# Gate and up projections of a feed-forward as seven products of half blocks, with the down projection moved behind them

## The chip, the cores and the metric

The kernel runs on one core of a Trainium2 chip. The metric is the device time of one execution in microseconds; the median of three runs is compared. All matrix products run on TensorE (PE in the profile), which takes a stationary operand of 128 x 128 and a moving one of up to 512 columns and adds into banks of PSUM. VectorE (DVE), ScalarE (ACT) and GpSimd (POOL) do the elementwise work, and the queue of SyncE (SP) issues the transfers between DRAM and SBUF.

## The reference

One layer of a streaming encoder over 1024 tokens of width 1024: two kinds of attention, a gated merge and an output projection, and then the feed-forward that this change is about:

```python
        merged = jax.nn.sigmoid(g_a) * y_a + jax.nn.sigmoid(g_b) * y_b
        x = x + rms_norm(merged @ w_o[l], ln_mix_post[l])

        h = rms_norm(x, ln_ffn_pre[l])
        f = (jax.nn.silu(h @ w_ffn_gate[l]) * (h @ w_ffn_up[l])) @ w_ffn_down[l]
        x = x + rms_norm(f, ln_ffn_post[l])
```

All of it is float32. The inner width of the feed-forward is 2816, 22 tiles of 128 (f tiles), and the model width is 8 tiles of 128 (k tiles).

## The kernel before

Every float32 matrix that is multiplied is held as two parts in a format that TensorE reads faster, a high and a low one. The high part is a cast on ACT (L252), the low part is what the cast left out, a subtract on POOL or DVE (L254); from PSUM it is L258 and L259. A product of two such matrices is three matmuls: high by high (L265), high by low (L266), low by high (L267). `load_hl` (L279) loads a matrix from DRAM (L283) and splits it.

The program runs in stages: norm and input projection, both attentions, `branch` a and b (projection of each attention, times its gate), `mix_out` (output projection and the two norms around it), then `ffn_gate_up` and `ffn_down`, and `finish` for each token tile. SBUF is one tensor AR for split parts and one tensor AFm for raw data; a `Zone` hands out places in them, of the free room the longest unused first. A scheduler orders each engine's queue; an instruction waits in its queue for what it reads and for the place that it writes.

`mix_out` goes over eight token tiles. One is 8 k tiles x 2 halves x 3 matmuls of 512 columns, and then a chain: sum of squares on ACT (L1062), reciprocal root (`rstd`: DVE L243, POOL L245), DVE L1064 and L1066, ACT L1069, `rstd` again, DVE L1071. The result is transposed on PE (L1085) and split into `h2`, the moving operand of the feed-forward. The transposes of a tile (the function `late`) are issued behind the matmuls of the next tile, and those of the last tile are handed to the feed-forward as `hook`, behind its first 48 matmuls.

`ffn_gate_up` works on a pair of f tiles (11 pairs). For each half of the tokens and each f tile it runs gate and up, 8 k tiles x 3 matmuls each, then Silu on ACT (L1116), the multiply on DVE (L1118) and a split into `aa`, which stays in SBUF. `ffn_down` multiplies `aa` of one or two such pairs with their rows of the down weights, 8 token tiles x 2 halves, and adds into a sum in SBUF (L1143, L1145). Gate and up of the next pair and down of the ones before alternate; the last group has four f tiles.

Of the kernel before, what the change touches and what calls it, by code (L numbers as in the profile page):

```python
# [65 lines left out]
MLA_DEPTH = 2  # L66

# [7 lines left out]
class Mem:  # L75
    """Columns of one SBUF tensor, handed out in program order."""
# [15 lines left out]
class Zone:  # L92
    """Windows of a Mem; of the room that is free there, the longest unused goes first."""
# [46 lines left out]
class Banks:  # L140
    """A window of PSUM banks; one bank, or an even and the next one, the longest unused first."""
# [27 lines left out]
def kernel(  # L169
# [46 lines left out]
    s_x1 = scratch("s_x1", (S, D))  # L216

# [19 lines left out]
    # ---------------------------------------------------------------- helpers  # L237
# [31 lines left out]
    class HL:  # L269
        """A matrix tile held as high and low parts: .h and .l of the given free shape."""  # L270
# [19 lines left out]
    # ------------------------------------------------------------ zones of phase one  # L290
# [18 lines left out]
    # ------------------------------------------------------------ phase 0: rotary tables  # L309
# [55 lines left out]
    def rope(src, t, nb, mid, dst):  # L365
        """dst = rope(src) for nb blocks of 64 columns; the tables of `mid` (q scaled, k plain, or both)."""
# [912 lines left out]
```

## Time and profile before

| | us |
|---|---|
| median of 3 runs | 2069.7 |
| lowest and highest | 2068.66, 2070.66 |
| span of the profiled execution, first to last instruction | 2069.1 |
| PE busy | 2027.3 |
| DVE, ACT, POOL busy | 1009.0, 784.5, 443.4 |
| wait of PE at the start of `mix_out` | 2.9 |
| waits of PE around the start of the feed-forward | 5.5 |

Of the profiled execution the span is what is given; it lies 0.6 us below the median of the runs. Busy times are sums over stages of different kinds: attention ends at about 1080 us, `branch` at about 1240, `mix_out` at about 1332, and the rest is the feed-forward. A matmul's printed duration (0.39 us for 512 columns) is longer than the distance between two starts, because consecutive matmuls overlap.

### The profile page before, as it was taken

How to read it: one execution, taken by the hardware profiler on the slowest of the kernel's cores; microseconds unless marked ns; L12 is line 12 of the kernel's file. 1: busy time of each engine (PE TensorE's matmuls, PEld its weight loads, DVE VectorE, ACT ScalarE, POOL GpSimd, SP SyncE). 2: the span in 40 equal slices, each digit the busy share in tenths (PEclk: the TensorE clock that was granted, in tenths of full speed). 3: DMA queues.
4: the chain of work that ended last, by engine and by line, in shares of the span. 5: the costliest groups of instructions: out<-in, count | busy, mean ns of one | idle time of the engine just before them, and what ended most of it. 6: DMA issues, size and time to landing. Idle time of an engine off the chain costs nothing.

```text
span 2069.1 us, 28932 instructions
## 1 busy us (share of the span) xinstructions
PE 2027.3 (98%) x10920; PEld 1762.1 (85%) x10920; DVE 1009.0 (49%) x2283; ACT 784.5 (38%) x1734; POOL 443.4 (21%) x559
## 2 busy tenths in 40 slices
PE   6999999999999999999999999999999999999998
PEld 6898999999898988988888887878888888888886
DVE  7756757766665667877733364412122221222115
ACT  5435445454544446666753332321211112111112
POOL 2000010200000022222121221332323323133225
PEclk9999999999999999999999999999999999999999
DMA  5212121120211131440335434210212112121114
GB/s 166 74 40 82 42 61 44 55 62 28 78 45 59 49 105 46 158 145 19 107 92 158 141 115 141 88 56 31 62 31 61 52 40 60 33 61 42 51 41 142
DMA packets 138987, 153.44 MB, mean 74 GB/s; under 512 B 12480, under 2 KB 116320, under 8 KB 138848
## 3 DMA queue, kind: packets, MB, share of 16 engines
q1 hardware_dynamic: 138848, 151.60, 23.7%
q8 instruction: 85, 1.39, 0.3%
q14 instruction: 54, 0.44, 0.1%
HBM read 119.00 MB, written 32.57 MB: 73 GB/s over the span
## 4 chain that ended last, share of the span: by engine, by line
PE 89%; DVE 3%; ACT 2%; issue 1%; DMA 1%; POOL 1%; POOLq 0%; DVEq 0%; SPq 0%; ACTq 0%
PE PS L265 26%; PE PS L267 26%; PE PS L266 26%; PE PS L702 3%; PE PS L604 3%; PE PS L920 2%; DVE AR L254 1%; POOL AR L254 1%; DVE nm L643 0%; PE PS L684 0%; ACT AFm L644 0%; ACT AR L252 0%; PE PS L685 0%; PE PS L587 0%; PE PS L747 0%
## 5 line engine op out<-in xcount | busy, mean ns | idle before, releaser
L265 PE MATMUL PS<-AR 128*128 128x512 f32 (+3 forms) x2920 | 1070.5, 368 | 2.9 <-ACT AR L252 1.3
L266 PE MATMUL PS<-AR 128*128 128x512 f32 (+3 forms) x2920 | 1058.6, 363 | 3.1 <-DVE AR L254 2.9
L267 PE MATMUL PS<-AR 128*128 128x512 f32 (+3 forms) x2920 | 1059.8, 364 | 1.1 <-POOL AR L254 1.1
L265 PEld LDWEIGHTS PS<-AR 128*128 128x128 f32 x2920 | 550.6, 189 | 82.3 <-ACT AR L258 3.9
L266 PEld LDWEIGHTS PS<-AR 128*128 128x128 f32 x2920 | 551.3, 189 | 74.5 <-DVE AR L254 3.4
L267 PEld LDWEIGHTS PS<-AR 128*128 128x128 f32 x2920 | 550.3, 189 | 71.9 <-POOL AR L254 1.5
L252 ACT CAST AR<-AFm 128x1024 fp32r<-128x1024 f32 (+5 forms) x366 | 236.9, 670 | 567.0 <-PE PS L266 247.3
L254 POOL TENSOR_TENSOR AR<-AFm,AR 128x1024 fp32r<-128x1024 f32 (+4 forms) x169 | 298.3, 1774 | 690.4 <-ACT AR L252 644.7
L1118 DVE TENSOR_TENSOR AFm<-AFm,PS 128x512 f32<-128x512 f32 x44 | 30.3, 688 | 440.4 <-PE PS L267 438.4
L258 ACT CAST AR<-PS 128x512 fp32r<-128x512 f32 (+3 forms) x336 | 143.3, 447 | 149.2 <-DVE AFm L383 75.5
L259 DVE TENSOR_TENSOR AR<-PS,AR 128x512 fp32r<-128x512 f32 (+3 forms) x336 | 164.3, 506 | 39.4 <-ACT AR L258 37.9
L254 DVE TENSOR_TENSOR AR<-AFm,AR 128x384 fp32r<-128x384 f32 (+4 forms) x197 | 131.0, 696 | 78.7 <-ACT AR L252 51.7
L644 ACT ACTIVATE AFm<-PS,nm 128x1024 f32<-128x1024 f32 (+3 forms) x192 | 142.7, 745 | 46.0 <-DVE nm L643 28.8
L643 DVE TENSOR_REDUCE nm<-PS 128x1 f32<-128x1024 f32 (+3 forms) x192 | 143.7, 752 | 3.2
L1145 DVE TENSOR_TENSOR AFm<-AFm,PS 128x512 f32<-128x512 f32 x144 | 99.0, 688 | 94.6 <-PE PS L267 94.6
L614 POOL CAST AR<-AR 128x128 fp32r<-128x128 f32 (+1 forms) x128 | 43.8, 342 | 455.7 <-PE PS L685 262.3
L702 PE MATMUL PS<-AR 128*128 128x256 f32 x640 | 95.0, 290 | 0.1
L604 PE MATMUL PS<-idf,AFm 128*128 128x128 f32 x576 | 88.6, 275 | 2.2 <-ACT AFm L736 1.1
L702 PEld LDWEIGHTS PS<-AR 128*128 128x128 f32 x640 | 82.1, 189 | 5.2 <-ACT AFm L644 2.3
L622 POOL MEMSET AR<- 128x256 f32 x64 | 22.4, 350 | 294.0 <-PE PS L267 198.9
L604 PEld LDWEIGHTS PS<-idf,AFm 128*128 128x128 f32 x576 | 66.9, 140 | 10.8 <-ACT AFm L946 4.3
L1116 ACT ACTIVATE AFm<-PS 128x512 f32<-128x512 f32 x44 | 26.3, 597 | 127.8 <-PE PS L267 127.8
(121 smaller groups left out, 1242.5 us busy)
## 6 DMA issues: line engine op xcount, KB each, us to landing
AFm<-in_w_in_dram SPq DMA_DIRECT2D x72, 192.0 KB
AFm<-in_w_ffn_gate_dram SPq DMA_DIRECT2D x22, 512.0 KB
AFm<-in_w_ffn_up_dram SPq DMA_DIRECT2D x22, 512.0 KB
AFm<-in_w_ffn_down_dram SPq DMA_DIRECT2D x22, 512.0 KB
AFm<-in_x_dram SPq DMA_DIRECT2D x16, 512.0 KB
AFm<-in_w_in_dram SPq DMA_DIRECT2D x32, 256.0 KB
s_gate<-AFm SPq DMA_DIRECT2D x32, 256.0 KB
AFm<-s_gate SPq DMA_DIRECT2D x16, 512.0 KB
```

Source lines behind the costliest of these rows:

```text
L252: nc.scalar.copy(h, src)
L254: e.tensor_tensor(out=l, in0=src, in1=f32v(h), op=ALU.subtract)
L258: nc.scalar.copy(h, src)
L259: nc.vector.tensor_tensor(out=l, in0=src, in1=f32v(h), op=ALU.subtract)
L265: nc.tensor.matmul(o, lhsT=sh, rhs=mh, start=first, stop=False)
L266: nc.tensor.matmul(o, lhsT=sh, rhs=ml, start=False, stop=False)
L267: nc.tensor.matmul(o, lhsT=sl, rhs=mh, start=False, stop=last)
L604: nc.tensor.transpose(tb.ap[:, q * P:(q + 1) * P], C[:, (g + q) * P:(g + q + 1) * P], idf)
L643: nc.vector.tensor_reduce(out=nm[:, m:m + 1], in_=src, axis=ax, op=ALU.max, negate=True)
L644: nc.scalar.activation(out=dst, in_=src, func=ACTF.Exp, bias=nm[:, m:m + 1], scale=1.0, accum_out=ss[:, m:m + 1])
L702: nc.tensor.matmul(sb.ap[:, p * 256:(p + 1) * 256], lhsT=qs.ap[:, m * 256 + v * P:m * 256 + v * P + P], rhs=slots[p]["kT"][:, m, :], start ...
L1145: nc.vector.tensor_tensor(out=acc, in0=acc, in1=pb.ap, op=ALU.add)
```

## The change

For a pair of f tiles of gate (or up), the product of weights and `h2` is seen as a product of 2 x 2 blocks: two f tiles by two halves of k, and two halves of k by two halves of the tokens. By Strassen's method in Winograd's form these blocks are multiplied in seven products of half size in place of eight, each of 4 k tiles x 3 matmuls of 512 columns; sums and differences of blocks are made before and after.

- The weight parts (`stationary_parts`): seven per pair and projection, four sums or differences of raw blocks (three on DVE, one on POOL) and seven splits (five subtracts on POOL, two on DVE). Six parts are made ahead of use.
- The moving parts (`moving_parts`): for each of four pairs of token tiles, four differences (three on DVE, one on POOL) and seven splits (three on POOL, four on DVE), made in `mix_out` once both tiles of a pair are transposed. `mix_out` takes the token tiles in the order 0, 4, 1, 5, 2, 6, 3, 7. A moving operand is now four runs of 128 columns that lie 7168 columns apart, since the parts of the four pairs stand behind one another.
- After the products: a copy from PSUM on ACT and five adds on DVE per block; Silu on ACT for gate, the multiply for up (one on DVE, three on POOL), and the result is stored to DRAM (`s_aa`).
- `ffn_down` runs after all pairs, in groups of 2, 4, 4, 4, 4 and 4 f tiles; it loads `s_aa` and the down weights and splits both.
- The transposes of the last token tile stand behind the first two products (24 matmuls). `branch` b splits its result in four pieces of 128 columns in place of two of 256. The places of several matrices in AR move.

The core of the diff (helpers move two lines down, so L265 to L267 are L267 to L269 after it):

```diff
-    z_oa, z_ob, z_pw, z_mt = slots(mr, (2, 10)), slots(mr, (10, 18)), slots(mr, (0, 2), (18, 19)), [slots(mr, (2 + 2 * q, 4 + 2 * q)) for q in range(4)]
+    z_oa, z_ob, z_pw = slots(mr, (2, 10)), slots(mr, (9, 11), (13, 19)), slots(mr, (0, 3))
+    z_mt = [slots(mr, (q, q + 2)) for q in (3, 5, 7, 11)]
...
-    z_wo, z_h2, z_ff = slots(mr, (10, 18)), slots(mr, (0, 8)), slots(mr, (8, 19))
+    z_wo = [slots(mr, (q, q + 1)) for q in (9, 10, 13, 14, 15, 16, 17, 18)]
+    z_wc, z_dn = Zone(mr, (28672, AR_COLS)), Zone(mr, (0, AR_COLS))
...
+        order = [t for p in range(4) for t in (p, p + 4)]
...
+            def flip():
                 for g in range(2):
                     tb = ps_a.alloc()
                     for i in range(4):
                         k = 4 * g + i
                         nc.tensor.transpose(tb.ap[:, i * P:(i + 1) * P], y.ap[:, k * P:(k + 1) * P], idf)
-                    split_psum(tb.ap.rearrange("p (k s) -> p k s", k=4), h2[:, 4 * g:4 * g + 4, 0, hs], h2[:, 4 * g:4 * g + 4, 1, hs])
+                    b = X.f.alloc(512)
+                    if g:
+                        nc.vector.tensor_copy(b.ap, tb.ap)
+                    else:
+                        nc.scalar.copy(b.ap, tb.ap)
...
+                if t >= 4:
+                    moving_parts(t - 4)
...
+        def moving_parts(p):
+            blk = Zone(mr, (7168 * p, 7168 * (p + 1))).alloc(7168, 7168)
+            v = blk.v("p (i h c) -> p i h c", i=7, h=2)
+            b11, b12, b21, b22 = raw.pop((0, 0)), raw.pop((0, 1)), raw.pop((1, 0)), raw.pop((1, 1))
...
+            put(MB["11"], b11, "pool")
+            put(MB["21"], b21, "dve")
+            t1 = diff(b12, b11, nc.vector)
+            t3 = diff(b22, b12, nc.gpsimd)
+            t2 = diff(b22, t1, nc.vector)
+            put(MB["t1"], t1, "pool")
+            put(MB["t3"], t3, "dve")
+            put(MB["22"], b22, "pool")
+            t4 = diff(b21, t2, nc.vector)
+            put(MB["t2"], t2, "dve")
+            put(MB["t4"], t4, "dve")
...
+    def stationary_parts(wt, g):
+        raw = f_ffn.alloc(2048)
...
+        yield part(A[0, 0], "pool")
+        s1, s1v = both(A[1, 0], A[1, 1], ALU.add, nc.vector)
+        s2, s2v = both(s1v, A[0, 0], ALU.subtract, nc.vector)
+        yield part(s2v, "pool")
+        yield part(s1v, "dve")
+        s3, s3v = both(A[0, 0], A[1, 0], ALU.subtract, nc.gpsimd)
+        yield part(s3v, "pool")
+        yield part(A[0, 1], "pool")
+        yield part(A[1, 1], "pool")
+        s4, s4v = both(A[0, 1], s2v, ALU.subtract, nc.vector)
+        yield part(s4v, "dve")
...
+        def product(bank, i, first):
+            X.fill()
+            w = X.parts.pop(0)
+            v = w.v("p (h k c) -> p h k c", h=2, k=4)
+            for k in range(4):
+                mh, ml = [X.h2v[:, :, i, h, k * P:(k + 1) * P] for h in range(2)]
+                o = bank.ap.rearrange("p (q s) -> p q s", q=4)
+                for x, (ws, m) in enumerate(((0, mh), (0, ml), (1, mh))):
+                    nc.tensor.matmul(o, lhsT=v[:, ws, k], rhs=m, start=first and k == 0 and x == 0,
+                                     stop=k == 3 and x == 2, skip_group_check=True)
...
+                product(a, MB["11"], True)
+                s1 = tmp()
+                nc.scalar.copy(s1.ap, a.ap)
+                product(b, MB["t2"], True)
+                u2 = add(s1, b)
+                product(c, MB["t1"], True)
+                product(b, MB["t3"], False)
+                u3 = add(s1, b)
+                c22 = add(u3, c)
+                done(1, 1, c22)
+                product(a, MB["21"], False)
+                done(0, 0, a)
+                product(b, MB["t4"], False)
+                c21 = add(s1, b)
+                done(1, 0, c21)
+                product(c, MB["22"], False)
+                c12 = add(u2, c)
+                done(0, 1, c12)
+
+    def ffn_down(X, f0, n):
+        aa, ws = [], []
+        for f in range(f0, f0 + n):
+            aa.append(load_hl(s_aa[f * P:(f + 1) * P, :], f_dn, z_dn, S))
+            ws.append(load_hl(w_d[f * P:(f + 1) * P, :], f_dn, z_dn, D, eng="dve"))
...
+    down = [ffn_down(X, 0, 2)] + [ffn_down(X, f0, 4) for f0 in range(2, NFF, 4)]
+    next(down[0])
+    for i, d in enumerate(down):
+        if i + 1 < len(down):
+            next(down[i + 1])
+        next(d, None)
```

How the instructions stand on three engines. First PE before the change, around the transposes of the last token tile (L1085), with feed-forward matmuls (L265 to L267) on both sides:

```order
L266 MATMUL PS<-AR 128x512
L267 MATMUL PS<-AR 128x512
L1085 MATMUL PS<-idf,AFm 128x128 [waits DVE_49]
L1085 MATMUL PS<-idf,AFm 128x128 x7
L265 MATMUL PS<-AR 128x512
L266 MATMUL PS<-AR 128x512
L267 MATMUL PS<-AR 128x512
```

The same place after it: the last matmuls of the output projection (L268, L269), the products (L1216) and the transposes of the last token tile (L1080).

```order
L268 MATMUL PS<-AR 128x512
L269 MATMUL PS<-AR 128x512
L1216 MATMUL PS<-AR 128x512 [waits Activation_49]
L1216 MATMUL PS<-AR 128x512 [waits Pool_49]
L1216 MATMUL PS<-AR 128x512 x10
L1216 MATMUL PS<-AR 128x512 [waits Activation_49]
L1216 MATMUL PS<-AR 128x512 [waits DVE_49]
L1216 MATMUL PS<-AR 128x512 x10
L1080 MATMUL PS<-idf,AFm 128x128 [waits DVE_49]
L1080 MATMUL PS<-idf,AFm 128x128 x7
L1216 MATMUL PS<-AR 128x512 [waits Activation_49]
```

There were 48 matmuls without a wait ahead of these transposes, and there are 24 now, in two products whose first two matmuls wait; the next product behind the transposes waits too.

On DVE the chain of the last token tile before the change, from L1064 to the first multiply of the feed-forward (L1118):

```order
L1064 SCALAR_TENSOR_TENSOR AFm<-PS,rs_r,AFm 128x1024 [waits Pool_49]
L259 TENSOR_TENSOR AR<-PS,AR 128x4x128 [waits Activation_49]
L1066 TENSOR_TENSOR AFm<-AFm 128x1024 [waits DMAHW5_49,DVE_49]
L243 TENSOR_SCALAR rs_v<-ss 128x1 [waits Activation_49]
L1071 SCALAR_TENSOR_TENSOR AFm<-AFm,rs_r 128x1024 [waits Pool_49]
L1118 TENSOR_TENSOR AFm<-AFm,PS 128x512 [waits PE_49,Activation_49]
```

And after it (L1065, L1067 and L1072 are the same three operations; L1180 are sums of raw weights, L1103 and L256 differences and subtracts of the moving parts, L1083 the copy of the transposed tile):

```order
L1065 SCALAR_TENSOR_TENSOR AFm<-PS,rs_r,AFm 128x1024 [waits PE_49,Pool_49]
L1067 TENSOR_TENSOR AFm<-AFm 128x1024 [waits DMAHW5_49,DVE_49]
L1180 TENSOR_TENSOR AFm<-AFm 128x512 [waits DMAHW1_49,DMAHW0_49]
L1180 TENSOR_TENSOR AFm<-AFm 128x512 [waits DVE_49]
L245 TENSOR_SCALAR rs_v<-ss 128x1 [waits Activation_49]
L1072 SCALAR_TENSOR_TENSOR AFm<-AFm,rs_r 128x1024 [waits Pool_49]
L1083 COPY AFm<-PS 128x512 [waits PE_49]
L1103 TENSOR_TENSOR AFm<-AFm 128x512 [waits Activation_49]
L1103 TENSOR_TENSOR AFm<-AFm 128x512 [waits DVE_49]
L256 TENSOR_TENSOR AR<-AFm,AR 128x512 [waits Activation_49]
```

Two sums, of which the first waits for transfers, stand in the chain of the last tile, and behind it the copy and the differences come before the first subtract.

On SP, in the middle of the feed-forward, one pair of f tiles after the change (before it, there were the same weight loads and in place of the stores two loads of down weights):

```order
L1242 DMA s_aa<-AFm 128x512 [waits DMAHW1_49,Pool_49]
L1168 DMA AFm<-in_w_ffn_up_dram 128x4x256 [waits DMAHW2_49,Pool_49]
L1242 DMA s_aa<-AFm 128x512 [waits DMAHW3_49,DVE_49]
L1242 DMA s_aa<-AFm 128x512 [waits DMAHW4_49,Pool_49]
L1242 DMA s_aa<-AFm 128x512 [waits DMAHW5_49,Pool_49]
L1168 DMA AFm<-in_w_ffn_up_dram 128x4x256 [waits DMAHW6_49,DVE_49,Pool_49]
L1168 DMA AFm<-in_w_ffn_gate_dram 128x4x256 [waits DMAHW7_49,Pool_49]
L1168 DMA AFm<-in_w_ffn_gate_dram 128x4x256 [waits DMAHW0_49,DVE_49,Pool_49]
```

Four stores stand among the four weight loads of a pair, and each load waits for POOL, which reads the raw weights that lie in its place.

## Rows read from the trace of the kernel before

**Rows 1.** The page: span, and busy time of each engine

```profile
span 2069.1 us, 28932 instructions
...
PE 2027.3 (98%) x10920; PEld 1762.1 (85%) x10920; DVE 1009.0 (49%) x2283; ACT 784.5 (38%) x1734; POOL 443.4 (21%) x559
```

**Rows 2.** The page: the chain that ended last, by engine

```profile
PE 89%; DVE 3%; ACT 2%; issue 1%; DMA 1%; POOL 1%; POOLq 0%; DVEq 0%; SPq 0%; ACTq 0%
```

**Rows 3.** Waits of PE: 1080 to 1330 us, then 1325 us to the end

```profile
PE PS L266 <- DVE AR L254: 2.9, 1, 2.9
...
PE PS L1085 <- DVE AFm L1071: 5.5, 2, 4.7
```

**Rows 4.** Windows of the feed-forward (columns in the first row)

```profile
core 0: us, PE busy (x) PEld busy (x) DVE busy (x) ACT busy (x) POOL busy (x), PEclk, DMA share, GB/s
1500.00:1600.00 100.00, 100.00 (x443) 82.84 (x442) 23.03 (x34) 15.65 (x20) 27.83 (x14) 1.00 0.16 48
...
1340.00:1380.00 40.00, 35.35 (x152) 29.10 (x151) 9.88 (x10) 9.31 (x14) 10.10 (x7) 0.91 0.19 59
```

**Rows 5.** Timeline of DVE: start us, us, engine, line, operation, idle before

```profile
1363.70 0.69 DVE L1118 TENSOR_TENSOR AFm<-AFm,PS 128x512 f32<-128x512 f32 x1 [9.67 <-PE PS L267]
1374.58 0.69 DVE L1118 TENSOR_TENSOR AFm<-AFm,PS 128x512 f32<-128x512 f32 x1 [10.19 <-PE PS L267]
```

**Rows 6.** Groups by shape, 1080 us to the end

```profile
L254 POOL TENSOR_TENSOR AR<-AFm,AR 128x512 fp32r<-128x512 f32 x44 | 56.7, 1288 | 283.8 <-ACT AR L252 282.1 <-DMA AFm<-in_w_ffn_down_dram 1.7
L1118 DVE TENSOR_TENSOR AFm<-AFm,PS 128x512 f32<-128x512 f32 x44 | 30.3, 688 | 440.4 <-PE PS L267 438.4 <-ACT AFm L1116 2.0
L252 ACT CAST AR<-AFm 128x512 fp32r<-128x512 f32 x44 | 27.3, 620 | 208.5 <-DVE AFm L1118 208.5
...
L1177 POOL TENSOR_TENSOR AFm<-AFm 128x512 f32<-128x512 f32 x14 | 20.9, 1515 | 6.1 <-DVE AFm L1176 6.1
...
L245 POOL TENSOR_TENSOR rs_r<-rs_v,mhalf 128x1 f32<-128x1 f32 x24 | 13.2, 550 | 78.3 <-DVE rs_v L243 78.3
...
L259 DVE TENSOR_TENSOR AR<-PS,AR 128x512 fp32r<-128x512 f32 x16 | 10.9, 684 | 0.9 <-ACT AR L258 0.9
...
L1064 DVE SCALAR_TENSOR_TENSOR AFm<-PS,rs_r,AFm 128x1024 f32<-128x1024 f32 x8 | 10.3, 1284 | 7.6 <-POOL rs_r L245 7.6
...
L1062 ACT ACTIVATE AFm<-PS 128x1024 f32<-128x1024 f32 x8 | 8.2, 1024 | 31.2 <-issue 16.5 <-PE PS L267 14.7
```

**Rows 7.** Timeline of DVE, token tiles of the output projection

```profile
1312.40 1.22 DVE L1066 TENSOR_TENSOR AFm<-AFm 128x1024 f32<-128x1024 f32 x1
...
1315.77 1.28 DVE L1071 SCALAR_TENSOR_TENSOR AFm<-AFm,rs_r 128x1024 f32<-128x1024 f32 x1 [0.73 <-POOL rs_r L245]
...
1346.12 3.35 DVE L1071 SCALAR_TENSOR_TENSOR AFm<-AFm,rs_r 128x1024 f32<-128x1024 f32 x1 [1.36 <-POOL rs_r L245]
```

**Rows 8.** Chain, 1325 to 1360 us: start us, us, what

```profile
1337.46 3.78 DMA AFm<-in_w_ffn_gate_dram
1341.31 1.06 ACT AR L252
...
1342.44 2.38 POOL AR L254
...
1346.12 3.37 DVE AFm L1071
...
1351.50 0.43 PE PS L265
```

**Rows 9.** Timeline of PE, last token tiles of the output projection

```profile
1308.32 1.04 PE L1085 MATMUL PS<-idf,AFm 128*128 128x128 f32 x8
...
1320.12 1.03 PE L1085 MATMUL PS<-idf,AFm 128*128 128x128 f32 x8
...
1331.66 0.39 PE L267 MATMUL PS<-AR 128*128 128x512 f32 x1
...
1349.53 1.97 PE L1085 MATMUL PS<-idf,AFm 128*128 128x128 f32 x8 [4.65 <-DVE AFm L1071]
```

More of the change, by code (lines that the diff above doesn't have):

```diff
@@ L66 @@
 MLA_DEPTH = 2
+AHEAD = 6
 AR_COLS = 38912
@@ L1038, in branch, with mix_out @@
             b.free()
-    def mix_out(X):
-        X.h2 = [None, None]
-        late = None
-        wo = [load_hl(w_o[k * P:(k + 1) * P, :], f_raw, z_wo, D, eng="dve" if k % 2 else "pool") for k in range(NK)]
+    def mix_out(X, prefetch):
+        X.h2 = []
+        wo = [load_hl(w_o[k * P:(k + 1) * P, :], f_raw, z_wo[k], D, eng="dve" if k % 2 else "pool") for k in range(NK)]
         mt = [b.v("p (d h s) -> p d h s", d=NK, h=2) for b in X.mt]
@@ L1047, in mix_out, with post @@
         nc.sync.dma_start(wf.ap, ln_ffn_pre[0].partition_broadcast(P))
[L1048 to L1049 removed]
+        banks = Banks(mp, 0, 6)
+        order = [t for p in range(4) for t in (p, p + 4)]
+        late, raw = [], {}
+        def post(t, pb, xt):
             rows = slice(t * P, (t + 1) * P)
[L1051 to L1059 removed]
             y = X.f.alloc(D, 1024)
@@ new lines, in mix_out @@
+        for n, t in enumerate(order):
+            p, hs = t % 4, slice((t // 4) * P, (t // 4) * P + P)
+            last = n == NT - 1
+            xt = X.f.alloc(D, 1024)
+            nc.sync.dma_start(xt.ap, x2d[t * P:(t + 1) * P, :])
+            pb = banks.alloc(2)
+            ks = (0, 1, 3, 4, 5, 6, 7, 2) if last else range(NK)
+            for x, k in enumerate(ks):
+                for c in range(2):
+                    sl = slice(c * 512, (c + 1) * 512)
+                    mm3(pb.ap[:, sl], mt[p][:, k, 0, hs], mt[p][:, k, 1, hs], wo[k].h[:, sl], wo[k].l[:, sl], x == 0, x == NK - 1)
+                if last:
+                    wo[k].free()
+                    if x == 1:
+                        late.pop(0)()
+                        late.pop(0)()
+                    if x in (3, 5, 6):
+                        prefetch()
+            if n % 2:
+                X.mt[p].free()
+            post(t, pb, xt)
+            if late and n < NT - 2 and len(late) > 1:
+                late.pop(0)()
@@ L1090, in mix_out @@
+        for f in late:
+            f()
         wp.free()
         wf.free()
[L1092 to L1128 removed]
@@ L1241, with prefetch, fill @@
     drain(branch(X, "b"))
-    last_h2 = mix_out(X)
-    X.gu, X.dn = Banks(mp, 0, 4), Banks(mp, 4, 8)
-    X.acc = [X.f.alloc(D, 1024) for _ in range(NT)]
-    prev = []
-    for g in range(NFF // 2):
-        cur = ffn_gate_up(X, g, last_h2 if g == 0 else None)
-        if prev and g < NFF // 2 - 1:
-            ffn_down(X, 2 * g - len(prev), prev)
-            prev = []
-        prev = prev + cur
-    ffn_down(X, NFF - len(prev), prev)
+    X.parts, stream = [], ffn_parts()
+    def prefetch():
+        X.parts.append(next(stream))
+    def fill():
+        while len(X.parts) < AHEAD:
+            b = next(stream, None)
+            if b is None:
+                return
+            X.parts.append(b)
+    X.fill = fill
+    mix_out(X, prefetch)
+    h2 = mr.ap[:, 0:28672]
+    X.h2v = h2.rearrange("p (q i h c) -> p q i h c", q=4, i=7, h=2)
+    ffn_gate_up(X)
+    for b in X.h2:
+        b.free()
+    X.dn = Banks(mp, 0, 8)
+    X.acc = [f_acc.alloc(D, 1024) for _ in range(NT)]
+    down = [ffn_down(X, 0, 2)] + [ffn_down(X, f0, 4) for f0 in range(2, NFF, 4)]
[4 more added lines that the diff above has]
+        next(d, None)
 _INS = ['x', 'positions', 'ln_mix_pre', 'w_in', 'lambda_q1', 'lambda_k1', 'lambda_q2', 'lambda_k2', 'da_subln',
```

144 lines of the change are left out of this document (82 added, 62 removed).

## The prediction

> **What bounds the kernel now.** I read the page first: TensorE is busy in 2027.3 of 2069.1 us [rows 1], and it is 89% of the chain that ended last [rows 2]. A saving therefore has to come out of TensorE's own work. The waits of PE were read next, since a saving is kept only where PE is not made to wait instead: from 1325 us to the end PE waits 5.5 us, all of it for the transposed last token tile, and between 1080 and 1330 us 2.9 us, at the start of the output projection [rows 3]. In the middle of the feed-forward the window of 1500 to 1600 us shows 443 matmuls at a granted clock of 1.00 (2.4 GHz), PE busy throughout, POOL 28% and DVE 23% [rows 4]. The reader is to see a stage with nothing on it but PE's pace, and engines beside it with more than two thirds of their time free.
>
> The pace comes from starts, not from the printed duration of one matmul, since consecutive ones overlap. A multiply on DVE follows every 48 matmuls: 1363.70 and 1374.58 are 10.88 us apart, so one matmul of 512 columns is 10.88/48 = 0.2267 us [rows 5].
>
> **Matmuls removed.** A pair of f tiles of one projection needed 4 x 8 x 3 = 96 matmuls; seven products of 4 x 3 are 84. Twenty-two such blocks (11 pairs, gate and up) save 22 x 12 = 264. The down projection keeps its 1056. 264 x 0.2267 = **-59.8 us**. The Trainium skill, TensorE: Matmul & The Clock Gate, section "Wait — 56ns, not 53.3ns?", gives 215.7 ns from start to start for 512 columns at the full clock; by it the saving would be 56.9 us. The row of this kernel decides, and the difference of 2.9 us lies inside my range.
>
> **The steady gate and up blocks.** A block is now 84 x 0.2267 = 19.04 us of PE. Its cover, per block, from the rows of the shapes [rows 6]: POOL five subtracts of 1.288 and one sum that I price at the 1.515 of an add with all operands in SBUF, 8.0 us, and for up three multiplies more, 12.5 us. DVE five operations in SBUF (two subtracts, three sums) and five adds from PSUM, each about 0.688, 6.9 us, for up one more. ACT seven casts of 0.620, a copy, and for gate four Silu, all priced like a cast, at most 7.4 us. None reaches 19.04 alone. The trace shows that a DVE operation with all operands in SBUF is held up by a POOL operation: L1071 takes 1.28 us alone and 3.35 us while POOL subtracts [rows 7]; the PSUM adds L1118 keep 0.688 on average [rows 6]. So POOL's time and DVE's 3.4 us in SBUF count as one resource: 11.4 us for gate, 15.9 us for up, still below 19.04. The weights are loaded two transfers at a time, in the order shown right after the previous projection's parts are made, about a block ahead; a transfer took 3.78 us to land [rows 8]. The four stores of 256 KB that stand between them on SP wait for multiplies that are done in the same block. I take **0** here; the bounds are 0 and the second rival below. If this cover were gone, the nearest price is DVE and POOL fully one after the other, 12.5 + 7.6 = 20.1 us for up, 1.1 us more than PE, 11 times: 12 us.
>
> **Branch b to output projection.** The weights of the output projection are loaded into places that the branch holds to its end, so the first of them is cast and subtracted after the last matmul of the branch. The same kind of wait is there now, 2.9 us [rows 3]. A cast and a POOL subtract of 1024 columns take 1.06 and 2.38 us [rows 8]; I take **+1**, bounds 0 and +3.4 - 2.9 + 1.5 = +2 (1.5 for one POOL operation in the way).
>
> **The eight token tiles of the output projection.** One takes 11.80 us (1308.32 to 1320.12): 48 matmuls, 10.88, and 0.92 for eight transposes [rows 9]. A tile's norm chain is needed one tile later and now has time to spare: L1071 ends at 1315.77 + 1.28 = 1317.05, the transposes start at 1320.12, 3.1 us later [rows 7, 9]. New beside it, per pair of tiles: on POOL three subtracts and a difference, 3 x 1.288 + 1.515 = 5.4 us; on DVE four subtracts and three differences, 7 x 0.688 = 4.8 us; on ACT seven casts, 4.3 us. The splits from PSUM that go (L259, 0.684 each) give back part of it. The chain has two DVE operations in SBUF and two short POOL ones; each can lose up to 1.3 us to a POOL subtract of 512 columns. Two such hits fit into 3.1 us, three don't. Three hits are 3.9, so up to about 0.8 a tile, and 1.5 a pair: bounds 0 and +6, taken **+3**.
>
> **Output projection to feed-forward.** Now PE loses 5.5 us of waits [rows 3], the transposes at 1349.53 take 1.97 instead of 0.92 [rows 9], and six matmuls after them, from 1351.50 on, start 0.43 instead of 0.227 apart (the lower level, 1.2 GHz), 1.2 us [rows 8], in a stretch in which the granted clock is 0.91 on average [rows 4]: 7.8 us. It is no more, because 48 feed-forward matmuls run before the last tile's transposes, whose chain ends only at 1349.49, some 17.4 us after that tile's last matmul (1331.66 + 0.39) [rows 8, 9]. In the changed order 24 matmuls stand there: products 11 and 21, which need token tiles 0 to 3 alone. They are 5.4 us. The chain of the last tile by itself is about 8.2 us: two reductions on ACT (1.02 and a read of 0.2 each), two POOL powers of 0.55, three DVE operations of 1.22 to 1.28, and 0.8 for the small ones between [rows 6, 7]. In the changed order two sums for weight parts (one waits for a transfer) stand before its L1072 on DVE, and splits stand on POOL: I add 4.5, so 12.7 - 5.4 = 7.3 us idle. Ahead of it products 11 and 21 wait for the parts of token tile 3 and for ACT's copy, about 2. Behind it the transposes lose 1.05, and then no product can go before its part is made of the transposed data: copy 0.6, difference 0.7, cast 0.62, subtract 1.29, 3.2 us. Slow matmuls as now, on more starts, 2. The first up weights, whose place is free only after these differences, 1.5. Together 17, less 7.8: **+9**. Bounds: chain undisturbed, 8.2 - 5.4 + 1.05 + 3.2 + 1.2 = 8.2, so 0; the chain as long as now, 12 + 1 + 1.05 + 3.2 + 3 + 4.5 = 24.8, so +17.
>
> **Gate and up to down.** The first two f tiles were stored some ten blocks before; their loads wait for room only, and in the order the first down matmul waits for casts whose data needs places that come free two products (5.4 us) before the end. Landing, cast and subtract are 3.78 + 1.06 + 2.38 = 7.2 [rows 8], so 1.8 us remain, less where the load is already there: **+1**, bounds 0 and +3. The first group (2 f tiles) then lasts 96 x 0.2267 = 21.8 us and covers the next eight loads; later groups last 43.5 us.
>
> The four runs of 128 columns in which parts are written cost nothing: L259 writes such runs in 0.684, L1118 one run in 0.688 [rows 6]. **Sum:** -59.8 + 1 + 3 + 9 + 0 + 1 = -45.8, so the span 2069.1 becomes 2023.3. The median of the runs is 2069.7, 0.6 above it: **2024 us**. All low bounds give 2010; all high bounds -59.8 + 2 + 6 + 17 + 3 = -31.8, 2038; with 8 us for the steady blocks 2046.
>
> **Rivals.**
> 1. *The moving operand is read slower.* Each matmul now takes it as four runs of 128 columns that lie 7168 columns apart. No matmul of the trace does so; the nearest row is a transpose, 0.92/8 = 0.115 us for 128 columns [rows 9]. Four of these are 0.46 us: 1848 x 0.233 = +431 us, about 2455, slower. It decides from 46/1848 = 0.025 us a matmul, a pace of 0.252. Against it: no other engine pays for such runs. By the Trainium skill, SBUF — State Buffer, section "Door 1: The DMA port swizzle", a stride costs only where successive accesses leave a 16-byte line, so runs of 512 bytes would be free; no run here shows it. Chance 0.05.
> 2. *DVE becomes late in the steady blocks.* The adds that empty a bank (u2, u3) must be over within one product, 12 x 0.2267 = 2.72 us, before the next product accumulates there. If one SBUF operation waits ahead of them for a POOL operation, that is 1.5 + 0.69 + 0.69 = 2.9, 0.2 too long; with two, 2.4 too long. Between 0.2 and 1 us on 44 adds is 9 to 44 us: 2033 to 2068. For it speaks the 3.35 us of L1071 [rows 7]. The Trainium skill, SBUF — State Buffer, section "Who interferes with whom", says so as a rule: of a DVE operation with two SBUF inputs and a GpSimd operation that reads SBUF, the second to issue blocks for the whole of the first; the trace agrees, 1.28 against 3.35. Against it: PSUM adds are not held up and POOL is free nearly half the time. Chance 0.13.
> 3. *The reload is not hidden:* loads of the first down groups start only when the last product is over. 7.2 us and a second pair of casts and subtracts, 3.4, about 11 us instead of 1: 2034. Chance 0.04, inside the range.
>
> **How the numbers follow.** The forecast has 0.78. Range 2009 to 2046: the low bounds, and the high ones with half of the second rival. Outside lie rival 1, the upper half of rival 2 (0.07) and some 0.06 of the forecast's own tails. A measurement here can tell about 0.2% (4 us) from no change. Slower: rival 1 and a little of rival 2, 0.06; within 0.2%: 0.01; faster 0.93.
>
> **What would show it.** Right: PE's matmuls at 0.227 apart in windows of the gate and up stage at full clock with 84 per block of 19.0 us; PE's waits of some 15 us between the last token tile and the third product, against 5.5; the down groups without waits. Wrong: starts 0.25 us or more apart in that stage (rival 1), waits of PE for L1225 in every block (rival 2), or a wait of over 3 us before the first down matmul (rival 3).

## The result, and the profile after

The changed kernel takes 2034.28 us in the median of four runs (2032.73 to 2036.90), against 2070.18 for the kernel before. The ratio is 0.9826, with an interval of 0.9812 to 0.984: 35.9 us less, where 45.8 were forecast; the time lies inside the range of 2009 to 2046. The profiled execution was the longest of the four, 2036.9 us with a span of 2035.0; what follows is measured on its span, 34.1 us shorter than before.

The first lines of the page, beside [rows 1]:

```profile
span 2035.0 us, 29108 instructions
...
PE 1976.3 (97%) x10656; PEld 1715.3 (84%) x10656; DVE 1156.2 (57%) x2464; ACT 864.2 (42%) x1912; POOL 541.0 (27%) x652
```

PE runs 10656 matmuls instead of 10920, the 264 that were counted. The windows of the start of the feed-forward and of a steady stretch, with the columns of [rows 4]:

```profile
1340.00:1370.00 30.00, 20.39 (x74) 15.37 (x75) 24.62 (x23) 13.01 (x23) 18.36 (x13) 0.83 0.16 53
1370.00:1400.00 30.00, 26.98 (x106) 21.33 (x105) 15.35 (x17) 11.44 (x19) 18.95 (x13) 0.89 0.30 90
1600.00:1700.00 100.00, 100.00 (x443) 82.81 (x442) 41.05 (x54) 32.58 (x54) 52.03 (x39) 1.00 0.24 74
```

In the steady stretch PE has the same 443 matmuls per 100 us as before, although POOL has gone from 28% to 52% and DVE from 23% to 41%. In the 60 us from 1340 on it is busy for 47, at a granted clock of 0.83 and 0.89. Where PE stood is told by its waits; the first fence is from 1080 to 1330 us, the second from 1330 us to the end, where [rows 3] had one line each:

```profile
PE PS L268 <- POOL AR L256: 3.7, 2, 2.4
PE PS L1080 <- DVE AFm L1072: 1.9, 2, 1.0
PE PS L269 <- POOL AR L256: 1.6, 1, 1.6
PE PS L1080 <- DVE rs_v L245: 1.3, 1, 1.3
PE PS L267 <- ACT AR L254: 1.1, 1, 1.1
```

```profile
PE PS L1080 <- DVE AFm L1072: 9.8, 2, 5.1
PE PS L1216 <- POOL AR L256: 4.9, 3, 3.0
PE PS L1216 <- ACT AFm L1249: 0.7, 1, 0.7
PE PS L1216 <- DVE AFm L1225: 0.3, 1, 0.3
PE PS L1216 <- DVE AR L256: 0.2, 1, 0.2
```

These are 25.5 us of waits against 8.4. By stages, from PE's starts in the two timelines (each stage from its first matmul to that of the next; the very first matmul starts at 11.8 us in both):

| stage | before | after | difference | forecast |
|---|---|---|---|---|
| up to branch b | 1135.35 | 1135.9 | +0.5 | 0 |
| branch b | 87.04 | 90.23 | +3.2 | +1, with its end |
| output projection | 99.53 | 109.79 | +10.3 | +3 |
| feed-forward to its last matmul | 725.8 | 677.7 | -48.1 | -59.8 + 9 + 0 + 1 |

In the feed-forward -59.8 is the matmuls, so +11.7 is lost. Of that 11.1 lie before 1405 us, 0.6 behind it, and none at the start of the down projection. From the last matmul's start to the end it is 9.6 us in both kernels. The 0.5 us ahead of branch b can't be told from zero: that stretch lasts 1133.5 to 1136.8 us in the experiments on the changed kernel.

### The profile page after: what moved, and what is told of

Read it like the earlier page. It is cut to its first block, busy times and chain, and to the rows that moved or that the text cites. A ratio compares the mean times of both kernels' runs of the same rounds, so it can differ in the third digit from the quotient of the medians.

```text
span 2035.0 us, 29108 instructions
## 1 busy us (share of the span) xinstructions
PE 1976.3 (97%) x10656; PEld 1715.3 (84%) x10656; DVE 1156.2 (57%) x2464; ACT 864.2 (42%) x1912; POOL 541.0 (27%) x652
## 5 line engine op out<-in xcount | busy, mean ns | idle before, releaser
L267 PE MATMUL PS<-AR 128*128 128x512 f32 (+3 forms) x2216 | 795.1, 361 | 4.0 <-ACT AR L254 2.5
L269 PE MATMUL PS<-AR 128*128 128x512 f32 (+3 forms) x2216 | 786.3, 356 | 2.6 <-POOL AR L256 2.6
L268 PE MATMUL PS<-AR 128*128 128x512 f32 (+3 forms) x2216 | 784.5, 355 | 3.7 <-POOL AR L256 3.7
L254 ACT CAST AR<-AFm 128x512 fp32r<-128x512 f32 (+4 forms) x514 | 301.7, 610 | 514.1 <-PE PS L1216 207.4
L267 PEld LDWEIGHTS PS<-AR 128*128 128x128 f32 x2216 | 418.1, 189 | 56.8 <-ACT AR L260 3.5
L268 PEld LDWEIGHTS PS<-AR 128*128 128x128 f32 x2216 | 419.0, 189 | 47.8 <-POOL AR L256 4.5
L269 PEld LDWEIGHTS PS<-AR 128*128 128x128 f32 x2216 | 417.9, 189 | 46.3 <-POOL AR L256 3.5
L256 POOL TENSOR_TENSOR AR<-AFm,AR 128x512 fp32r<-128x512 f32 (+4 forms) x203 | 309.2, 1529 | 461.7 <-ACT AR L254 397.4
L1216 PE MATMUL PS<-AR 128*128 128x512 f32 x1848 | 425.7, 392 | 6.1 <-POOL AR L256 4.9
L1216 PEld LDWEIGHTS PS<-AR 128*128 128x128 f32 x1848 | 349.3, 189 | 82.2 <-POOL AR L256 6.2
L256 DVE TENSOR_TENSOR AR<-AFm,AR 128x512 fp32r<-128x512 f32 (+5 forms) x311 | 213.1, 714 | 109.3 <-ACT AR L254 81.8
L260 ACT CAST AR<-PS 128x512 fp32r<-128x512 f32 (+3 forms) x320 | 134.5, 440 | 149.5 <-DVE AFm L388 75.4
L1225 DVE TENSOR_TENSOR AFm<-AFm,PS 128x512 f32<-128x512 f32 x110 | 75.2, 684 | 180.3 <-PE PS L1216 179.6
L261 DVE TENSOR_TENSOR AR<-PS,AR 128x512 fp32r<-128x512 f32 (+3 forms) x320 | 152.9, 496 | 38.0 <-ACT AR L260 36.5
L1180 DVE TENSOR_TENSOR AFm<-AFm 128x512 f32<-128x512 f32 x66 | 70.4, 1066 | 68.4 <-DMA s_aa<-AFm 29.7
```

The costliest lines, as they stand in the source:

```text
L254: nc.scalar.copy(h, src)
L256: e.tensor_tensor(out=l, in0=src, in1=f32v(h), op=ALU.subtract)
L260: nc.scalar.copy(h, src)
L261: nc.vector.tensor_tensor(out=l, in0=src, in1=f32v(h), op=ALU.subtract)
L267: nc.tensor.matmul(o, lhsT=sh, rhs=mh, start=first, stop=False)
L268: nc.tensor.matmul(o, lhsT=sh, rhs=ml, start=False, stop=False)
```

## The experiments

Ratios are to the kernel before, run beside it on the same chip. "Loss" of a stage is what its timeline has beyond 0.2267 us for each step from one matmul to the next. A transpose counts as a step too, though it takes 0.115 us, so each eight of them lower the loss by 0.9 and a stage can come out below zero; only differences of it are read. For the changed kernel it is 3.2 in branch b, 10.0 in the output projection, 17.2 in the first two blocks, and for the kernel before 0.0, -0.2 and 6.1 (start of the feed-forward).

Theory A after the result: PE's new waits come from DVE operations with all operands in SBUF that stand still while POOL works in SBUF, and from POOL's own queue ahead of its powers. Rival B: the amount of work beside the chain. Rival C: late transfers and places. One more possibility was not set against A: the same subtract of 512 columns takes 0.685 us on DVE and 1.29 on POOL, so moving it to DVE shortens it by itself. It can't explain a shorter wait for the norm chain, from which nothing is moved, but it stands beside A wherever PE waits for a moved subtract.

**e1, the moving parts on DVE**

```diff
-            put(MB["11"], b11, "pool")
+            put(MB["11"], b11, "dve")
...
-            t3 = diff(b22, b12, nc.gpsimd)
+            t3 = diff(b22, b12, nc.vector)
...
-            put(MB["t1"], t1, "pool")
+            put(MB["t1"], t1, "dve")
...
-            put(MB["22"], b22, "pool")
+            put(MB["22"], b22, "dve")
```

> All subtracts and differences of the moving parts run on DVE, none on POOL. Theory A (a DVE operation with all operands in SBUF stands still while POOL works, and the chain's two POOL powers stand behind POOL's subtracts): the waits of PE for transposes inside the output projection, 7.9 us in the changed kernel (1.31, 0.89, 0.96 and 4.72), fall to 2 to 4 us although DVE gets 2.8 us more work per pair of tiles, and the time falls by 3 to 6 us, to about 2029. Rival B (the amount of work beside the chain counts, not where it runs): DVE is fuller, the waits stay at 8 us or grow, 2034 to 2038.

2025.03 us, ratio 0.9791 (0.9777 to 0.9806). The loss in the output projection falls from 10.0 to 3.5 us, and the waits for transposes there from 7.9 to 2.7, with more work on DVE. That is theory A, and B falls for this stage. (A has two parts, DVE held up by POOL and the powers behind POOL's subtracts; this run takes both away at once.) A new wait of 5.6 us came inside the first product, before its second matmul, for three subtracts on DVE beside POOL.

**e2, the moving parts one token tile later**

```diff
-                    moving_parts(t - 4)
+                    todo.append((t - 4, [raw.pop(k) for k in ((0, 0), (0, 1), (1, 0), (1, 1))]))
...
             post(t, pb, xt)
+            while todo:
+                moving_parts(*todo.pop(0))
```

> The moving parts of a pair are written one token tile later in the program, behind the norm chain of the next tile. Theory A and rival B alike: the chain of token tile 3 no longer meets the parts of the third pair, so its transposes wait less than 2 us instead of 4.7; but those parts now meet the last tile's chain, and the products wait longer. 2030 to 2037, no clear gain. Rival C (late transfers and places, not the moving parts, hold the chain up): nothing changes at token tile 3.

2030.00 us, ratio 0.9814 (0.9799 to 0.9828). As expected the loss moved: 3.4 in the output projection, 19.6 in the first two blocks, with a wait of 5.5 us for POOL inside the first product. The time is not told from that of the changed kernel, and since A and B expected the same, only C is weakened.

**e3, most moving parts left out** (four differences and five of seven splits are missing)

```diff
             put(MB["21"], b21, "dve")
-            t1 = diff(b12, b11, nc.vector)
...
-            put(MB["t4"], t4, "dve")
-            t4.free()
+            for b in (b11, b12, b21, b22):
+                b.free()
```

> Of each pair only the parts 11 and 21 are made; the four differences and the five other splits are left out, so five of the seven products multiply old data of the same size. If the moving parts cause the loss in the output projection (A and B): the transposes wait under 1.5 us in all, and the wait of the third product behind the last transposes goes: 2034 less 6 less 3, about 2024. Rival C: waits of 4 us or more stay in the output projection, about 2030.

2015.91 us, ratio 0.9747 (0.9732 to 0.9762). The first two blocks lose 1.0 us, but the output projection still 7.5. My expectation for that stage was wrong: the wait at token tile 3 is as long as ever. Timeline rows of e3, of PE, POOL and DVE:

```profile
1336.33 1.94 PE L1080 MATMUL PS<-idf,AFm 128*128 128x128 f32 x8 [4.37 <-DVE AFm L1072]
...
1329.38 1.34 POOL L256 TENSOR_TENSOR AR<-AFm,AR 128x512 fp32r<-128x512 f32 x1 [0.35 <-ACT AR L254]
...
1333.84 7.63 POOL L256 TENSOR_TENSOR AR<-AFm,AR 128x512 fp32r<-128x512 f32 x5
...
1329.50 2.31 DVE L1067 TENSOR_TENSOR AFm<-AFm 128x1024 f32<-128x1024 f32 x1
...
1333.90 2.28 DVE L1072 SCALAR_TENSOR_TENSOR AFm<-AFm,rs_r 128x1024 f32<-128x1024 f32 x1 [0.73 <-POOL rs_r L247]
```

Two operations of the chain take 2.3 us instead of 1.2 and 1.28, because POOL now subtracts the first weight parts at this place. Waits of over 4 us in this stage were what I had expected of rival C; the rows show why they are not for it: POOL's work stretches the chain, whether or not it is for the moving parts.

**e4, the first up weights in the place of the gate weights**

```diff
-        raw = f_ffn.alloc(2048)
+        raw = (Zone(mf, (0, 2048)) if g == 0 else f_ffn).alloc(2048)
```

> The raw up weights of the first pair of f tiles take the place of the gate weights (columns 0 to 2047) instead of one that is held by the moving parts. If the late place cost what the profile shows (a wait of 3.0 us before the first up product at 1380 us and 13 matmuls at the lower clock level behind it, 2.9 us), the time falls by 5 to 6 us, to 2029. Rival: the up parts are late because POOL and DVE are full, and the wait comes back at the same product: 2033 to 2035.

2042.59 us, ratio 0.9875 (0.9859 to 0.9892), slower than the changed kernel. The wait of 3.0 us at 1380 us is gone; PE waits 1.9 us for POOL and 2.5 for ACT earlier in the stretch instead, and the first two blocks lose 14.2 instead of 17.2. But the places of all later pairs are exchanged too, and the down weights find theirs late: behind the first one (1758.8 us) the next two loads go out only behind the last store, at 1788.8 us (the second row, SP), where in the changed kernel they did at 1768.9. SP, then PE:

```profile
1788.44 0.32 SPq L1242 DMA_DIRECT2D s_aa<-AFm  x1
1788.81 0.91 SPq L285 DMA_DIRECT2D AFm<-in_w_ffn_down_dram  x2
```

```profile
1795.97 1.65 PE L267 MATMUL PS<-AR 128*128 128x512 f32 x3 [5.92 <-ACT AR L254]
```

PE runs 24 down matmuls and then waits 5.9 us, and the down stage loses 8.1 us with the slow matmuls behind the wait. The loss in the steady blocks rose to 4.1 as well: PE waits 2.2 us at 1410.1 us for an add of DVE, and the add stands in DVE's queue behind a sum of raw weights that waits 3.3 us until a store has ended. That is a late place again:

```profile
1408.52 0.90 DVE L1180 TENSOR_TENSOR AFm<-AFm 128x512 f32<-128x512 f32 x1 [3.27 <-DMA s_aa<-AFm]
1409.35 0.68 DVE L1225 TENSOR_TENSOR AFm<-AFm,PS 128x512 f32<-128x512 f32 x1
```

**e5, also the first pair's weight parts on DVE** (on top of e1)

```diff
+        pe, pv = ("dve", nc.vector) if g == 0 else ("pool", nc.gpsimd)
-        yield part(A[0, 0], "pool")
+        yield part(A[0, 0], pe)
...
-        s3, s3v = both(A[0, 0], A[1, 0], ALU.subtract, nc.gpsimd)
-        yield part(s3v, "pool")
+        s3, s3v = both(A[0, 0], A[1, 0], ALU.subtract, pv)
+        yield part(s3v, pe)
```

> As e1, and the parts of the first pair of f tiles (gate and up) are made on DVE too, so that POOL has only its powers and nothing that stands against DVE from the output projection to the second pair. Theory A: the wait of 5.6 us before the first product in e1 (three DVE subtracts took 5.17 us instead of 2.1 beside POOL) falls to about 2.5 us; the whole falls by 3 to 5 us below e1, a ratio of 0.977. Rival B (the amount of work on DVE counts): DVE gets 10 operations of 0.69 more in this stretch, and the waits grow; ratio 0.979 to 0.982.

2019.05 us, ratio 0.9751 (0.9737 to 0.9766). The first two blocks lose 9.9 us instead of 15.2 (e1), the wait inside the first product is down to 1.9. Ten operations more on DVE made the stretch shorter: B falls here too, and it fits theory A, but the moved subtracts are also shorter on DVE (0.68 us against 1.72 on POOL in this stretch of the changed kernel), and the two are not separated. The wait of 3.0 us for the first up parts is gone without any change of place: the last wait on POOL (1.1 us at 1351.8 us) comes before the up weights are even loaded, and behind it PE waits for nothing until 1378.9 us. Rows of PE and SP:

```profile
1351.81 26.07 PE L1217 MATMUL PS<-AR 128*128 128x512 f32 x105 [1.10 <-POOL AR L256]
...
1354.79 0.93 SPq L1168 DMA_DIRECT2D AFm<-in_w_ffn_up_dram  x2
```

**e6, the first up weights in a place of their own**

```diff
-            for wt in (w_g, w_u):
-                yield from stationary_parts(wt, g)
+            for wt, lo in ((w_g, 0), (w_u, 11264 if g else 2048)):
+                yield from stationary_parts(wt, g, lo)
```

> The changed kernel with another place for the raw up weights of the first pair alone (columns 2048 to 4095, free since the output weights were split); all later pairs keep the places that they have. If the late place is the cause: the wait of 3.0 us before the first up product and the 13 slow matmuls behind it go, 5 to 6 us, ratio 0.980; the start of the down projection stays without a wait, other than in e4. Rival (DVE and POOL are full there): the wait moves to another product and the ratio stays at 0.982 to 0.983.

2037.01 us, ratio 0.9839 (0.9822 to 0.9855): no gain. The wait for the up parts went, and two waits of 2.9 and 2.6 us came behind the last transposes, so the first two blocks still lose 15.6:

```profile
1361.52 1.22 PE L1217 MATMUL PS<-AR 128*128 128x512 f32 x2 [2.94 <-ACT AR L254]
1365.34 8.34 PE L1217 MATMUL PS<-AR 128*128 128x512 f32 x25 [2.60 <-POOL AR L256]
```

So the place had held that product up, and yet nothing was gained: the rival's sign came, the wait moved. In the changed kernel 14 matmuls follow the last transposes at once and cover the parts that are made there; here only two matmuls run between the two waits, so the edit also changed what stands where on PE, and the run alone does not tell the full queues from that. The edit also kept temporaries out of the first 4096 columns, which I had taken for harmless; behind 24 down matmuls PE waits 4.6 us here and the down stage loses 7.5.

**e7, e5 and e6 together**

> e5 and e6 together. If the two causes are separate, their gains add: e1 was 43 us below the kernel before, with another 4 and 5 us it is 52 below, ratio 0.975. If both gains are the same one (DVE's and POOL's queues in the stretch between the stages), ratio 0.977 to 0.979.

2024.24 us, ratio 0.9780 (0.9766 to 0.9795). No sum of gains: the first two blocks lose 9.2 against 9.9 in e5, and the down stage 6.6. The stages say so and not the ratio, which these 6.6 us have brought from one expectation to the other.

**e8, also the output weights on DVE** (on top of e7)

```diff
-z_wo[k], D, eng="dve" if k % 2 else "pool")
+z_wo[k], D, eng="dve")
```

> e7, and the output weights are split on DVE alone instead of on POOL and DVE in turns. Theory A: at the start of the output projection two adds of branch b on DVE (2.4 us each instead of 0.69) stood beside two POOL subtracts of 2.56 us; without POOL these and the waits of 2.4 and 1.3 us shrink by 2 to 3 us in all, ratio 0.001 below e7. Rival C (the output weights come late because their places are held to the end of branch b): the wait stays, same ratio as e7.

2022.17 us, ratio 0.9770 (0.9756 to 0.9785). The loss in the output projection goes from 1.8 to -1.6, in branch b from 2.7 to 1.9; that in the first two blocks rises from 9.2 to 10.0, in the down stage from 6.6 to 7.5. The intervals of e7 and e8 overlap, so a gain in time is not shown, only that of the stage.

**e9, e5 with the output weights on DVE**

> e5 with the output weights split on DVE alone, without the moved place of e6. Theory A: the gain of e8 over e7 in the output projection (the sum of waits and slow starts there fell from 1.8 to -1.6 us, and by 0.8 in branch b) comes here too, and the start of the down projection stays without a wait: e5's ratio of 0.9751 less 4 us, 0.973, about 2015 us. If the gain of e8 came from the moved place, 0.975.

2016.15 us, ratio 0.9748 (0.9734 to 0.9761). The profile has the stage's gain (2.1 to -0.9 in the output projection, 2.8 to 2.0 in branch b), the times of e5 and e9 don't tell the two apart, and by its ratio alone the other expectation, 0.975, would be met. What the DVE operations cost between 1236 and 1390 us, groups by shape, first the changed kernel, then e9:

```profile
L256 DVE TENSOR_TENSOR AR<-AFm,AR 128x512 fp32r<-128x512 f32 x20 | 19.9, 1004 | 0.3
L1103 DVE TENSOR_TENSOR AFm<-AFm 128x512 f32<-128x512 f32 x12 | 15.0, 1247 | 0.1
L1072 DVE SCALAR_TENSOR_TENSOR AFm<-AFm,rs_r 128x1024 f32<-128x1024 f32 x8 | 12.3, 1533 | 4.8 <-POOL rs_r L247 4.8
...
L1035 DVE TENSOR_TENSOR AFm<-AFm 128x512 f32<-128x512 f32 x2 | 4.8, 2458 | 0.0
...
L1225 DVE TENSOR_TENSOR AFm<-AFm,PS 128x512 f32<-128x512 f32 x5 | 3.4, 681 | 5.8 <-PE PS L1216 5.8
```

```profile
L256 DVE TENSOR_TENSOR AR<-AFm,AR 128x512 fp32r<-128x512 f32 x45 | 31.4, 729 | 0.2
...
L1103 DVE TENSOR_TENSOR AFm<-AFm 128x512 f32<-128x512 f32 x16 | 11.8, 753 | 0.0
L1072 DVE SCALAR_TENSOR_TENSOR AFm<-AFm,rs_r 128x1024 f32<-128x1024 f32 x8 | 10.3, 1284 | 4.5 <-POOL rs_r L247 4.5
...
L1035 DVE TENSOR_TENSOR AFm<-AFm 128x512 f32<-128x512 f32 x2 | 1.4, 685 | 0.0
```

The same instruction (L1035) takes 2.46 us on average beside POOL's subtracts and 0.685 without them; e9's 61 subtracts and differences of 512 columns cost 43 us, and at the means of the changed kernel they would cost 65. The add from PSUM (L1225) keeps 0.68: in the changed kernel 53 of its 110 adds overlap POOL's work, and they take 0.683 us like the other 57. The delay stands in an operation's own duration and not in the idle time before it.

**e10, the steady blocks' parts all on POOL** (on top of e9)

```diff
+        de, dv = ("dve", nc.vector) if g == 0 else ("pool", nc.gpsimd)
...
-        s1, s1v = both(A[1, 0], A[1, 1], ALU.add, nc.vector)
+        s1, s1v = both(A[1, 0], A[1, 1], ALU.add, dv)
...
-        yield part(s1v, "dve")
+        yield part(s1v, de)
```

> e9, but from the second pair of f tiles on all parts of gate and up are made on POOL: seven subtracts of 1.29 and four sums of 1.5 for a block, and the three multiplies of up, 15.0 us for gate and 19.6 us for up against 19.04 us of matmuls. This takes the cover away that I counted on. By the rows POOL's mean of 17.3 us still fits and parts are made six ahead: same as e9 within 2 us. If a block must fit by itself, 0.6 us and more are lost in each of ten up blocks, 6 to 15 us.

2015.50 us, ratio 0.9741 (0.9728 to 0.9754), the same as e9. A steady window of e10:

```profile
1600.00:1700.00 100.00, 100.00 (x443) 82.81 (x442) 19.82 (x29) 30.24 (x50) 82.56 (x67) 1.00 0.25 85
```

POOL is at 83% and PE has no gap, so all parts can be made on POOL. Whether only the mean has to fit is not shown: POOL's sums take 1.29 us here, not the 1.5 of my expectation (from 1400 to 1700 us),

```profile
L1180 POOL TENSOR_TENSOR AFm<-AFm 128x512 f32<-128x512 f32 x64 | 82.3, 1292 | 12.1 <-DMA AFm<-in_w_ffn_up_dram 10.1 <-DMA AFm<-in_w_ffn_gate_dram 0.8
```

and with subtracts and multiplies of 1.29 too an up block is 14 x 1.29 = 18.1 us, below 19.04: each block fits by itself.

**e11, order of two loads in branch b** (on top of e9)

```diff
-        ot = load_ot(src, z_oa if which == "a" else z_ob)
+        gen = load_ot(src, z_oa if which == "a" else z_ob)
+        ot = [next(gen) for _ in range(NK if which == "a" else NK - 1)]
...
             w = load_cols(X, wt, d * P)
+            ot.extend(gen)
```

> e9, and in branch b the last of the eight loads of the attention output is written behind the first weight load. If the wait of 1.6 us at the start of branch b (the low part of its first weights) came from this queue order, it goes, and the time falls by 1 to 1.6 us below e9. If it comes from a place, nothing changes.

2013.81 us, ratio 0.9734 (0.9720 to 0.9747). The wait at the start of branch b, still 0.4 us in e9, is gone and branch b loses 1.3 instead of 2.0. That is little to go by: with the old order this wait is 0.2 to 0.4 us in e8 to e10 and 0.7 to 1.6 in the runs before them, which don't touch branch b. The intervals of e9 and e11 overlap, so a gain in time is not shown. It is the fastest of all by its median.

**e12, the kernel before with the same work on DVE**

```diff
-f_raw, z_wo, D, eng="dve" if k % 2 else "pool")
+f_raw, z_wo, D, eng="dve")
...
-f_raw, z_ff, 1024, "p (k c) -> p k c", k=4))
+f_raw, z_ff, 1024, "p (k c) -> p k c", eng="pool" if g > 1 else "dve", k=4))
```

> The kernel before the change, with the output weights and the first two pairs of feed-forward weights split on DVE alone, as e9 does. It tells which part of e9's gain has nothing to do with the seven products. Theory A (POOL holds DVE up wherever both work on SBUF): the wait of 2.9 us at the start of the output projection falls to about 1.1, the last L1071 takes 1.28 instead of 3.35 us and the wait of 4.65 us before the last transposes falls to under 2; 2062 to 2066, a ratio of 0.997 to 0.998. If POOL's share was no cause: ratio 1.000.

2058.42 us, ratio 0.9950 (0.9936 to 0.9963), 10.2 us less and twice what I expected. Waits of PE from 1080 us to the end, and the window from 1340 to 1380:

```profile
PE PS L1085 <- DVE AFm L1071: 0.9, 1, 0.9
PE PS L266 <- DVE AR L254: 0.2, 1, 0.2
```

```profile
1340.00:1380.00 40.00, 39.82 (x180) 33.12 (x181) 5.31 (x8) 10.71 (x15) 12.30 (x7) 1.00 0.19 59
```

The last L1071, 3.35 us before [rows 7], is down to

```profile
1338.84 1.29 DVE L1071 SCALAR_TENSOR_TENSOR AFm<-AFm,rs_r 128x1024 f32<-128x1024 f32 x1 [0.73 <-POOL rs_r L245]
```

The waits fall from 8.4 to 1.1 us. With them go the stretches at the lower clock level: the granted clock is 1.00 where it was 0.91 [rows 4], and behind the last transposes no matmuls start 0.43 apart. The wait at the start of the output projection falls from 2.9 to 0.2. So a good part of what e9 gains over the changed kernel (some 16 to 18 us) is no part of the seven products: the kernel before gains 10 us by the like edit. Against e12, e9 is some 42 us faster.

## Why the prediction was right, and where it was off

**Matmuls and pace: right.** 264 fewer, and from 1404.8 to 1786.3 us the 1680 matmuls of twenty blocks are 0.2271 apart on average. The first rival (four runs of 128 columns read slower) is out. The line rule that I cited for it from the Trainium skill (SBUF — State Buffer, "Door 1: The DMA port swizzle") agrees with the trace, 0.227 against a break-even of 0.252.

**Steady blocks: right.** 0.6 us lost in twenty blocks, no bank waits longer than 0.5 us, and e10 shows how much room was left. The second rival did not come in the changed kernel; one late add of its kind cost 2.2 us in e4, but behind a place and not behind POOL.

**Start of the down projection: +1 forecast, 0 measured.** The third rival is real all the same: where down weights of the first group are cast late, behind loads that stand after the last stores (e4, e6, e7, e8), 6.6 to 8.1 us are lost, against 10 forecast for it.

**Output projection to feed-forward: +9 forecast, +11.1 measured.** That the sum of 17 us came so near to 17.2 is luck, since its parts are otherwise divided. PE in the changed kernel:

```profile
1360.62 1.97 PE L1080 MATMUL PS<-idf,AFm 128*128 128x128 f32 x8 [5.13 <-DVE AFm L1072]
1362.41 5.11 PE L1216 MATMUL PS<-AR 128*128 128x512 f32 x14
1368.48 0.97 PE L1216 MATMUL PS<-AR 128*128 128x512 f32 x3 [0.95 <-POOL AR L256]
1369.63 7.78 PE L1216 MATMUL PS<-AR 128*128 128x512 f32 x33 [0.18 <-DVE AR L256]
1380.43 7.78 PE L1216 MATMUL PS<-AR 128*128 128x512 f32 x20 [3.02 <-POOL AR L256]
```

It is 5.1 us idle before the last transposes instead of 7.3. Behind them 1.1 us of waits stand where I had 3.2, because matmuls go on at once: that no product can run before its part is made of the last tile was wrong. But at the third matmul of the first up product, which reads the low part, there are 3.0 us of waiting and some 3 of slow starts where I had 1.5. I had given the lateness of the up weights to their place. The place has its share, as their wait goes where it is moved (e6), but nothing is gained by that; in e5 the place stays and the wait goes as well, with all parts of the first pair on DVE. So the elementwise work of this seam is the limit. Whether its parts were late because DVE and POOL hold each other up or because POOL's subtract is the longer one is not separated.

**Branch b: +1 forecast, +3.2 measured.** I had only costed its end. There PE waits 1.1, 2.4 and 1.25 us for output weights, where it waited 2.9: +1.9 against bounds of 0 and +2. (Only the 1.1 lies in the table's row of branch b, so 0.8 of the +10.3 below belongs here.) The wait of 1.6 us at its beginning, for the low part of its first weights, is not in the sum; its cause stays open, with e11 a hint at the order of the loads.

**The eight token tiles: +3 forecast, bounds 0 and +6, +10.3 measured.** This is the step that failed, in two places; the time stays within the range only because the other terms stayed below their high bounds. "A tile's norm chain is needed one tile later and now has time to spare: ... 3.1 us" does not hold for token tile 3: its transposes stand inside the last tile, behind 12 and 21 matmuls and eight transposes, 8.4 us for a chain of 8.2 us; 4.7 of the stage's 7.9 us of waits for transposes are its. And "each can lose up to 1.3 us" priced a hit, where every operation beside POOL's work is lengthened and the powers queue behind POOL as well. Timeline of that chain in the changed kernel, DVE, then POOL, then PE:

```profile
1332.55 1.22 DVE L1067 TENSOR_TENSOR AFm<-AFm 128x1024 f32<-128x1024 f32 x1
...
1334.29 2.89 DVE L1103 TENSOR_TENSOR AFm<-AFm 128x512 f32<-128x512 f32 x2
1337.10 0.14 DVE L245 TENSOR_SCALAR rs_v<-ss 128x1 f32<-128x1 f32 x1
...
1339.29 2.28 DVE L1072 SCALAR_TENSOR_TENSOR AFm<-AFm,rs_r 128x1024 f32<-128x1024 f32 x1 [0.44 <-POOL rs_r L247]
...
1336.59 1.71 POOL L256 TENSOR_TENSOR AR<-AFm,AR 128x512 fp32r<-128x512 f32 x1
1338.26 0.99 POOL L247 TENSOR_TENSOR rs_r<-rs_v,mhalf 128x1 f32<-128x1 f32 x1
...
1341.72 1.65 PE L1080 MATMUL PS<-idf,AFm 128*128 128x128 f32 x8 [4.72 <-DVE AFm L1072]
```

Two differences of 0.69 take 2.89 together ahead of L245, the power starts 1.0 us late behind POOL's subtract, L1072 takes 2.28: PE waits 4.7 us and goes on at the lower clock level. e1 took the moving parts off POOL and the loss of the stage fell to 3.5, near to what I had forecast. I had the row for it [rows 7] and made a rival of it for the steady blocks, where there is room; for the stage in which there is none I took only hits on the chain's own operations from it. The Trainium skill's rule on the shared port (SBUF — State Buffer, "Who interferes with whom") agrees with these rows: operations with two SBUF inputs wait for POOL, adds from PSUM don't.

Not settled: how e1's gain divides between DVE and the powers, and what of e9's remaining 9.8 us in the first two blocks could still be hidden.

## What to carry to other kernels

A fused change of the arithmetic pays in the steady stage at PE's full pace, and is paid for at its seams: list for each seam what must be done between the last matmul that feeds it and the first that needs it, and count the matmuls in between in the new order. In such a seam splitting elementwise work over POOL and DVE can be slower than giving all of it to DVE; in a steady stage with parts made ahead and room on both engines the division made no difference here (e10). A change of places in a shared pool can move a load at the other end of the program, so look at every stage after it.

## What the runs showed of the hardware that was not expected

- A DVE subtract or add of 512 columns with all operands in SBUF took 0.685 us alone and 2.46 us on average, in two cases, beside two POOL subtracts of 1024 columns; the same operation reading PSUM kept 0.68.
- The kernel before became 10.2 us faster when such work went from POOL to DVE (e12), although POOL was busy for only 21% of its span. How much of that is the delay and how much DVE's shorter subtract is not shown.
- A moving operand of four runs of 128 columns, 7168 columns apart, cost nothing: 443 matmuls per 100 us as with one run.
- In e12 the granted clock stayed at 1.00 (2.4 GHz) where PE's longest wait was 0.9 us; before, after a wait of 4.65 us, six matmuls started 0.43 us apart.
